# Second output projection of a two-layer decoder trunk: new chunk order, held-back slab sums, and four heads' causal masks moved to another engine

## The chip, the core and the metric

The kernel runs on one core of a Trainium2 chip. The engines of the core work side by side: PE multiplies matrices (its weight loads are listed apart as PEld), DVE is the vector engine, ACT the scalar engine, POOL a third elementwise engine, SP issues most DMAs. Each engine works through its own list of instructions in a fixed order, and an instruction waits until what it reads and overwrites is ready. The metric is the device time of one launch in microseconds (us). A smaller number is better.

## The reference

The model has two layers over 256 tokens of width 2048. The layer that matters here is the second:

```python
sk1, sk2, sv = shared_kv(x, kv_norm, w_kv, k_norm, cos, sin)   # 12 heads, two key maps each, values of 128
u = rms_norm(x, mix_norm[1]) @ w_in[1]
q1, q2 = ...                     # 12 heads of 64: normed, partly rotated
o = differential_attention(q1, q2, sk1, sk2, sv, lam)  # softmax(q1 k1) - lam * softmax(q2 k2), causal, times v
token_out = rms_norm(o, subln_norm[0]) * (1 - lam_init)
mem_out = memory_cross_attention(u[..., 1536:], mem, ...)      # 4 heads of 128, softmax over 256 memory rows
x = x + concatenate([token_out, mem_out]) @ w_out[1]
x = x + squared_relu_mlp(rms_norm(x, ffn_norm[1]), w_ff1[1], w_ff2[1])
```

So the output projection has 16 chunks of 128 input columns: chunks 0 to 11 come from the 12 differential heads, chunks 12 to 15 from the 4 memory heads.

## The kernel before, in words

All weights are float32 and come from HBM once. Every block of weights is split on the core into a rounded high part (ACT, line 157) and the rest (DVE, line 158), and a product is made of three reduced-precision products: high times high and high times low in one matmul of 512 columns (L391), low times high in one of 256 columns (L393). Two rings of six slots (`hi_ring`, `lo_ring`) hold the split blocks. A slot takes four blocks, and it is filled again only after the matmuls of the four blocks before have read it. `Feed` fixes the order of blocks; the split of a later block stands at its place in the fixed lists of ACT and DVE, up to three jobs ahead. Before each feed-forward stage the first slab of the second weight matrix gets sums of two raw tiles (L182 and L183 on DVE); they stand in the list `KOFF` = 2 jobs before the slab.

Work beside the projections is put off by a count of ticks: `at(d, fn)` runs `fn` after `d` ticks, and one tick is four weight blocks. A scheduler then orders each engine's list.

A differential head has four steps. `scores` makes two score tiles (`s1` for the second 128 queries, `s0` for the first), masks, maximum and exponentials. `turn` transposes the weights through bank `t` (`dt`, L1226). `pv` multiplies by the values into bank `o` (`do`, L1232 to L1234) and starts a chain: squares on ACT (L1242), a mean on DVE (L300 `o_v`), two small ACT functions (L359, L360), three small DVE operations ending in `o_y`, and the scaling L1250 on DVE, in two halves. `back` transposes the scaled result (`o_t`, L1255, in two halves) and writes the head's chunk of `cat1`. In the last four heads (8 to 11) `by_pe` is true: the causal mask is added to the scores by PE, as a bf16 matmul with the identity (L1189, L1193), and `pv` first copies the result out of its bank (L1237). The other heads add the mask on DVE (L1202, L1203) and scale straight out of the bank.

A memory head has `scores` (`ms`, L573), a maximum (L575, L576), exponentials on ACT (L579), a reciprocal and a scaling (L584, L586), a turn (`mt`, L592), a copy (L595), `pv` (`mo`, L600) and its chunk of `cat1` in two writes (ACT L601, DVE L602). The score tiles of all heads share two banks; there is one bank `t`, one bank `o`, and there are three banks for the tiles of the projections (tag `mm`).

`out_tiles` makes the 16 output tiles. The first three (called wo0, wo1 and wo2 here) get their chunks in parts while heads are still at work: in the second layer chunks 0 to 7, then 8 to 11, then 12 to 15. Each part runs over the three tiles. A tile's bank is free for the tile three later when `resid_add` (L638, L639) has read it.

Of the kernel before, what the change touches and what calls it, by code (L numbers as in the profile page):

```python
# [19 lines left out]
T = 256  # L20
# [35 lines left out]
class Plan:  # L56
# [7 lines left out]
    def __init__(self):  # L64
        self.entries = []
        self.npos = 0
        self.jobs = []
        self.slabs = []
# [37 lines left out]
class Feed:  # L106


    def __init__(self, nc, wst, wpool, rows, plan, dry):
        self.nc, self.wst, self.wpool, self.rows = nc, wst, wpool, rows  # L110
        self.plan, self.dry = plan, dry
        self.pos = 0
        self.slab_no = 0
        self.lp = self.pp = 0
        self.raw = {}
        self.split = {}
        self.t1 = None
        if not dry:
            self.hi = wpool.tile([P, SLOTS * 512], F32R, name="hi_ring")
            self.lo = wpool.tile([P, SLOTS * 512], F32R, name="lo_ring")  # L120
            self.busy = [False] * SLOTS
            self.at = 0
# [39 lines left out]
    def _prepare(self, p):  # L162
        sub, add = self.nc.vector.tensor_sub, self.nc.vector.tensor_add
        self.load(self.plan.need[p] + 1 + LOADS)
        if p[0] == "N":
            r = ("N", p[1] // 2)
            c = p[1] % 2 * 512
            if not self._split(p, self.raw[r][:, c : c + 512], 1):
                return False
            if c:  # L170
                del self.raw[r]
            return True
        ra, rb = self.raw[("S", p[1], 0)], self.raw.get(("S", p[1], 1))
        t1 = self.t1[1 if p[1] % 32 > 28 else p[1] % 2]

        def both():
            t2 = rb[:, 0:512].unsqueeze(1).to_broadcast([P, 2, 512])
            two = ra.rearrange("p (a c) -> p a c", a=2)
            sub(two, t2, two)

        if p[0] in "KL":
            add(t1, ra[:, 0:512], rb[:, 0:512])  # L182
            sub(rb[:, 0:512], t1, rb[:, 512:1024])  # L183
            if p[0] == "L":
                both()
            return True
        src, n = ((ra, 2), (t1, 1), (rb, 2), (ra, 2))[p[2]]
        if not self._split(p, src, n):
            return False
        if p[2] == 0 and ("K", p[1]) in self.plan.need:  # L190
            both()
        if p[2] == 3:
            del self.raw[("S", p[1], 0)], self.raw[("S", p[1], 1)]
        return True
# [68 lines left out]
def program(ctx, tc, plan, dry, xT, memT, par, lam, cst, wst, yT):  # L263
    nc = tc.nc
    cp = ctx.enter_context(tc.tile_pool(name="cp", bufs=1))
    sp = ctx.enter_context(tc.tile_pool(name="sp", bufs=1))
    wp = ctx.enter_context(tc.tile_pool(name="wp", bufs=1))
    tp = ctx.enter_context(tc.tile_pool(name="tp", bufs=1))
    pp = ctx.enter_context(tc.tile_pool(name="pp", bufs=1, space=PSUM))

    nc.scalar.preload_act_table_set("natural_log_exp_and_others")
    feed = Feed(nc, wst, wp, tp, plan, dry)

    acc = {}

# [20 lines left out]
    def mmt(name):  # L296
        return pp.tile([P, 512], F32, tag="mm", bufs=3, name=name)
# [8 lines left out]
    resid = cp.tile([P, NK, T], F32, name="resid")  # L306
# [70 lines left out]
    def a_part(ps, w, l, n, ks, xs, first=True, last=True, between=None):  # L377


        ks = list(ks)  # L380
        i = 0
        while i < len(ks):
            if between:
                between(i)
            two = []
            for k in ks[i : i + 2 - feed.pos % 2]:
                two.append((i, k % NK, *feed.block((w, l, k, n, 1))))
                feed.used()
                i += 1
            for c, k, hi, lo in two:  # L390
                nc.tensor.matmul(ps, hi, xs[:, k, :], start=first and c == 0, stop=False)  # L391
            for c, k, hi, lo in two:
                nc.tensor.matmul(  # L393
                    ps[:, T : 2 * T], lo, xs[:, k, 0:T], start=False,
                    stop=last and c == len(ks) - 1,
                )
            if feed.pos % 4 == 0:
                tick()
# [53 lines left out]
    def key_rows(ps, cols, d):  # L452

        n = 512 // d
        raw = tp.tile([P, 2, 512], F32, tag="rows", bufs=3, name="krow")
        v = tp.tile([P, 2, n], F32, tag="w16", bufs=6, name="kv")
        for t in range(2):
            nc.scalar.activation(raw[:, t, :], ps[t], AF.Copy, scale=cols[0][:, t : t + 1])
            sq = tp.tile([P, 512], F32, tag="rowsq", bufs=1, name="ksq")
            nc.scalar.activation(sq, raw[:, t, :], AF.Square)  # L460
            nc.vector.tensor_reduce(
                out=v[:, t, :], in_=sq.rearrange("p (h d) -> p h d", d=d), axis=AX.X, op=ALU.add
            )
        v = v.rearrange("p t n -> p (t n)")
        nc.vector.tensor_scalar(out=v, in0=v, scalar1=1.0 / d, scalar2=EPS, op0=ALU.mult, op1=ALU.add)
        y = tp.tile([P, 2 * n], F32, tag="w16", bufs=6, name="ky")
        rsqrt_cols(y, v)
        for t in range(2):
            rows = raw[:, t, :].rearrange("p (h d) -> p h d", d=d)
            yb = y[:, t * n : t * n + n].unsqueeze(2).to_broadcast([P, n, d])  # L470
            nc.vector.tensor_mul(rows, rows, yb)
        return raw
# [163 lines left out]

    def resid_add(ps, n):
        nc.vector.tensor_add(resid[:, n, :], resid[:, n, :], ps[:, 0:T])  # L638
        nc.vector.tensor_add(resid[:, n, :], resid[:, n, :], ps[:, T : 2 * T])  # L639

    def resid_done(n, splits, square=True):
        for dst, g in splits:
            split_gain(dst[:, n, :], resid[:, n, :], gcol(g + n))
        if square:
            add_square("x", resid[:, n, :], n == 0)
# [312 lines left out]
    ps = [mmt("mq0"), pp.tile([P, 512], F32, tag="o", bufs=1, name="mq0")]  # L958
# [14 lines left out]
    for h in range(4):  # L973
        mem_head(
            mq0[:, h, :], y0.rearrange("p (t h) -> p t h", t=2)[:, :, h], mk[:, h, :],
            lambda mb, h=h: mv[:, mb, h * P : h * P + P], ebuf[h % 2], pTb, cat[:, 12 + h, :],
# [51 lines left out]
    def out_tiles(l, cat, lead, ks, fx, between):  # L1028

        first = [mmt("wo") for _ in range(3)]  # L1030
        for i, part in enumerate(lead):
            for n in range(3):
                a_part(first[n], "w_out", l, n, part, cat, first=i == 0, last=False)
        between()
        for n in range(NK):
            if n < 3:
                ps = first[n]
                a_part(ps, "w_out", l, n, ks, cat, first=False)
            else:
                ps = mmt("wo")  # L1040
                a_part(ps, "w_out", l, n, sum(lead, []) + ks, cat)
            resid_add(ps, n)
            resid_done(n, [(fx, G_FFN + 16 * l)])

    group_u(3)
# [50 lines left out]
    def pair_of_banks(c, name):  # L1096
        if c % 2:
            return [pp.tile([P, 512], F32, tag="s", bufs=2, name=name) for _ in range(2)]
        return [mmt(name) for _ in range(2)]
# [3 lines left out]
    for c in range(3):  # L1103
        ps = pair_of_banks(c, "k1")
        b_tile(ps, "w_kv", 0, c, x_kv)
        rows = key_rows(ps, c1, 64)
# [8 lines left out]
    for c in range(3):  # L1115
        ps = pair_of_banks(c + 1, "v1")
# [9 lines left out]
    ps = pair_of_banks(0, "mk1")  # L1126
# [4 lines left out]
    ps = pair_of_banks(1, "mv1")  # L1131
# [7 lines left out]
    def carve(n):  # L1139
        off[0] += n  # L1140
        return att[:, off[0] - n : off[0]]
# [5 lines left out]
    pT1 = carve(512).rearrange("p (a t) -> p a t", a=2)  # L1147

    qb = [[carve(512).rearrange("p (m t) -> p m t", m=2) for _ in range(2)] for _ in range(3)]
    em1 = carve(512).rearrange("p (a t) -> p a t", a=2)  # L1150
# [22 lines left out]
    cat1 = sp.tile([P, NK, 512], F32R, tag="S1", name="cat1")  # L1173
# [90 lines left out]
    for c in range(3):  # L1264
        ps = pair_of_banks(0, "q1")
        b_tile(ps, "w_in_q", 1, c, x_mx)
        rows, v = query_rows(ps, c1, 64)
        rope(rows, qtab)
        y = query_scale(v, c1)
        for i in range(2):  # L1270
            j = 2 * c + i
            q = qb[j % 3]
            at(4 + i, lambda i=i, q=q, rows=rows: turn_queries(rows, 2 * i, q))
            for g in range(2):
                h = 2 * i + g

                diff_head(
                    2 * j + g, q[g], y, *((6 + 4 * h, 8, 4 if c == 0 else 3) if c < 2 else (6 + 2 * h, 6, 3)), c == 2
                )
    for h in range(4):  # L1280
        ps = mmt("mq1")
        c_tile(ps, "w_in", 1, 12 + h, range(NK), x_mx)
        q, y = mem_query(ps[:, 0:T], mqg1, c1)
        mem_head(
            q, y, mk1[:, h, :], lambda mb, h=h: mv1[:, mb, h * P : h * P + P],
            em1, pT1, cat1[:, 12 + h, :], 3,
        )

    fx1 = sp.tile([P, NK, 512], F32R, tag="S0", name="fx1")
    out_tiles(1, cat1, [list(range(8)), list(range(8, 12))], list(range(12, 16)), fx1, flush)  # L1290

    down = ffn(1, fx1, ("S2", "S1"), lambda n: nc.sync.dma_start(yT[:, n, :], resid[:, n, :]))
    down()
# [83 lines left out]
```

## Time and profile before

| | |
|---|---|
| time, median of 3 runs | 2045.21 us (2045.16 to 2045.78) |
| the profiled execution: time | 2044.93 us |
| the profiled execution: span of the profile | 2043.1 us |
| PE busy in the span | 2037.2 us |
| DVE, ACT busy in the span | 1716.2 us, 1349.8 us |

The span runs from the first to the last instruction of the program; 1.83 us of the profiled execution lie outside it. The busy time of PE contains overlaps of neighbouring matmuls and gaps that the modelled ends hide. What a matmul costs is therefore read from start to start: the start of the next minus its own.

### The profile page before, as it was taken

Reading aid. Unit: us, or ns where it says so; the run is one execution under the profiler, and the core shown is the slowest. Engines: PE = TensorE matmul, PEld = TensorE weight load, DVE = VectorE, ACT = ScalarE, POOL = GpSimd, SP = SyncE. Lnnn points to the kernel's source line nnn. Section 1 sums busy time; section 2 is a strip of 40 time slices with the busy share of each in tenths; the row PEclk is TensorE's granted clock in tenths of the full one; section 3 lists DMA queues with packets and bytes.
Section 4 is the critical chain, followed back from the end, with each engine's and each line's share of the span. In section 5 each row is a group of like instructions: output and inputs, shape, how many; then the busy total and the mean of one; then the engine's idle time right before and its main releaser. Section 6 shows DMA issues by size and latency. Waiting matters only on the chain.

```text
span 2043.1 us, 32257 instructions
## 1 busy us (share of the span) xinstructions
PE 2037.2 (100%) x11060; PEld 1755.3 (86%) x11060; DVE 1716.2 (84%) x3215; ACT 1349.8 (66%) x2505; POOL 51.9 (3%) x67
## 2 busy tenths in 40 slices
PE   9999999999999999999999999999999999999999
PEld 8888888888888888888888888888888888888888
DVE  8888889889879978999766687889879978988997
ACT  7765566666666756768665697566657666666764
POOL 0001200000000000000000000310000000000000
PEclk9999999999999999999999999999999999999999
DMA  9556556555555555655565543656555555565564
GB/s 314 178 181 190 188 174 206 197 196 197 186 201 202 189 207 191 207 169 182 194 228 186 170 140 103 196 166 207 196 196 205 186 196 196 186 210 195 196 209 135
DMA packets 110470, 390.75 MB, mean 191 GB/s; under 512 B 12256, under 2 KB 14944, under 8 KB 110304
## 3 DMA queue, kind: packets, MB, share of 16 engines
q1 hardware_dynamic: 110160, 388.59, 57.1%
q8 instruction: 86, 1.41, 0.3%
q14 instruction: 80, 0.66, 0.1%
q10 hardware_dynamic: 144, 0.10, 0.0%
HBM read 386.54 MB, written 2.10 MB: 190 GB/s over the span
## 4 chain that ended last, share of the span: by engine, by line
PE 99%; ACT 1%; DVE 1%; issue 0%
PE x_bank L391 33%; PE x_bank L393 16%; PE wo L391 6%; PE p L746 5%; PE p L747 5%; PE p L748 5%; PE wo L393 3%; PE u L391 2%; PE ff L391 2%; PE u L393 1%; PE k L417 1%; PE k L419 1%; PE v L417 1%; PE k L418 1%; PE v L419 1%; PE v L418 1%
## 5 line engine op out<-in xcount | busy, mean ns | idle before, releaser
L157 ACT CAST hi_ring<-raw 128x512 fp32r<-128x512 f32 x1193 | 736.7, 620 | 529.5 <-PE x_bank L391 308.0
L158 DVE TENSOR_TENSOR lo_ring<-raw,hi_ring 128x512 fp32r<-128x512 f32 x1193 | 817.2, 695 | 206.7 <-ACT hi_ring L157 165.5
L391 PE MATMUL x_bank<-fx,hi_ring 128*128 128x512 f32 x1920 | 602.1, 395 | 0.0
L393 PEld LDWEIGHTS x_bank<-fx,lo_ring 128*128 128x128 f32 x1920 | 361.0, 188 | 83.6
L393 PE MATMUL x_bank<-fx,lo_ring 128*128 128x256 f32 x1920 | 377.4, 278 | 0.0
L391 PEld LDWEIGHTS x_bank<-fx,hi_ring 128*128 128x128 f32 x1920 | 301.4, 189 | 9.3
L391 PE MATMUL x_bank<-z,hi_ring 128*128 128x512 f32 x960 | 301.1, 395 | 0.0
L158 DVE TENSOR_TENSOR lo_ring<-slab,hi_ring 128x1024 fp32r<-128x1024 f32 x188 | 230.1, 1224 | 54.3 <-ACT hi_ring L157 53.6
L157 ACT CAST hi_ring<-slab 128x1024 fp32r<-128x1024 f32 x188 | 196.9, 1047 | 73.1 <-PE x_bank L391 36.2
L393 PEld LDWEIGHTS x_bank<-z,lo_ring 128*128 128x128 f32 x960 | 180.5, 188 | 41.7
L393 PE MATMUL x_bank<-z,lo_ring 128*128 128x256 f32 x960 | 188.8, 278 | 0.0
L391 PE MATMUL wo<-cat,hi_ring 128*128 128x512 f32 x512 | 162.5, 398 | 0.5 <-DVE resid L639 0.5
L391 PEld LDWEIGHTS x_bank<-z,hi_ring 128*128 128x128 f32 x960 | 151.9, 189 | 6.5 <-ACT room L672 0.4
L393 PEld LDWEIGHTS wo<-cat,lo_ring 128*128 128x128 f32 x512 | 95.9, 188 | 21.7
L672 ACT COPY room<-x_bank 128x512 f32<-128x512 f32 x180 | 104.9, 583 | 2.0 <-PE x_bank L393 2.0
L393 PE MATMUL wo<-cat,lo_ring 128*128 128x256 f32 x512 | 101.4, 279 | 0.0
L746 PE MATMUL p<-hi_ring,sit 128*128 128x512 f32 x256 | 100.5, 393 | 0.0
L747 PE MATMUL p<-hi_ring,sit 128*128 128x512 f32 x256 | 100.2, 391 | 0.0
L748 PE MATMUL p<-lo_ring,sit 128*128 128x512 f32 x256 | 99.7, 389 | 0.0
L391 PEld LDWEIGHTS wo<-cat,hi_ring 128*128 128x128 f32 x512 | 79.1, 189 | 2.2 <-PE wo L393 0.9
L717 ACT ACTIVATE room<-room 128x256 f32<-128x256 f32 x128 | 53.2, 416 | 39.1 <-DVE room L300 39.1
L746 PE MATMUL p<-hi_ring,z 128*128 128x512 f32 x192 | 75.2, 392 | 0.0
(313 smaller groups left out, 3102.3 us busy)
## 6 DMA issues: line engine op xcount, KB each, us to landing
raw<-in_w SPq DMA_DIRECT2D x595, 512.0 KB, 4.0
slab<-in_w SPq DMA_DIRECT2D x124, 512.0 KB, 3.3
resid<-in_x SPq DMA_DIRECT2D x8, 256.0 KB, 5.9
room<-in_w SPq DMA_DIRECT2D x4, 512.0 KB, 4.2
memraw<-in_mem SPq DMA_DIRECT2D x4, 512.0 KB, 3.6
out_y<-resid SPq DMA_DIRECT2D x16, 128.0 KB, 1.8
memraw<-in_mem SPq DMA_DIRECT2D x7, 256.0 KB, 6.3
raw<-in_w SPq DMA_DIRECT2D x3, 256.0 KB, 3.5
```

What stands on the lines that cost most here:

```text
L157: self.nc.scalar.copy(hi, src)
L158: self.nc.vector.tensor_sub(lo, src, hi.bitcast(F32))
L391: nc.tensor.matmul(ps, hi, xs[:, k, :], start=first and c == 0, stop=False)
L393: nc.tensor.matmul(ps[:, T : 2 * T], lo, xs[:, k, 0:T], start=False, stop=last and c == len(ks) - 1,)
L417: nc.tensor.matmul(ps[t], xl, hi, start=k == 0, stop=False)
L418: nc.tensor.matmul(ps[t], xh, hi, start=False, stop=False)
L419: nc.tensor.matmul(ps[t], xh, lo, start=False, stop=k == NK - 1)
L672: nc.scalar.copy(x, ps)
L717: at(3, lambda: nc.scalar.activation(stage[i % 8], y[:, 0:T], AF.Square))
L746: nc.tensor.matmul(ps, a[1], hi, start=first, stop=False)
L747: nc.tensor.matmul(ps, a[0], hi, start=False, stop=False)
L748: nc.tensor.matmul(ps, a[0], lo, start=False, stop=last)
```

## The change

Four things are changed.

- The last four heads add their causal mask on DVE like the others (`by_pe` false). The 16 bf16 mask matmuls and the four copies L1237 go; eight mask additions of DVE come.
- The ticks of the last heads and of the memory heads are other: `pv` of heads 8 to 11 comes 7 ticks after their scores (before: 6), the scores of a memory head come after 4 ticks (before: 3) and its `pv` 7 ticks after those (before: 6).
- The chunks of wo0, wo1 and wo2 in the second layer come as 0 to 7, then 12, 8, 9, 13, then 10, 11, 14, then 15.
- The sums L182 and L183 of the first slab of each feed-forward stage are held, by a dependency for the scheduler alone, behind the second addition `resid_add` of the third output tile, in both layers.

```diff
@@ Feed._prepare
         if p[0] in "KL":
-            add(t1, ra[:, 0:512], rb[:, 0:512])
+            one = add(t1, ra[:, 0:512], rb[:, 0:512])
+            if self.gate:
+                self.tc.add_manual_dep(
+                    one.ins, self.gate,
+                    mybir.DependencyInfo(
+                        mybir.DependencyClass.NoSync, mybir.DependencyReason.SCHED_ONLY
+                    ),
+                )
+                self.gate = None
             sub(rb[:, 0:512], t1, rb[:, 512:1024])
@@ resid_add
-        nc.vector.tensor_add(resid[:, n, :], resid[:, n, :], ps[:, T : 2 * T])
+        return nc.vector.tensor_add(resid[:, n, :], resid[:, n, :], ps[:, T : 2 * T])
@@ out_tiles
-            resid_add(ps, n)
+            done = resid_add(ps, n)
+            if n == 2 and not dry:
+                feed.gate = done.ins.name
@@ the differential heads
-                    2 * j + g, q[g], y, *((6 + 4 * h, 8, 4 if c == 0 else 3) if c < 2 else (6 + 2 * h, 6, 3)), c == 2
+                    2 * j + g, q[g], y, *((6 + 4 * h, 8, 4 if c == 0 else 3) if c < 2 else (6 + 2 * h, 7, 3)), False
@@ the memory heads
-            em1, pT1, cat1[:, 12 + h, :], 3,
+            em1, pT1, cat1[:, 12 + h, :], 4, 7,
@@ the second output projection
-    out_tiles(1, cat1, [list(range(8)), list(range(8, 12))], list(range(12, 16)), fx1, flush)
+    out_tiles(1, cat1, [list(range(8)), [12, 8, 9, 13], [10, 11, 14]], [15], fx1, flush)
```

The lists of SP and POOL are the same in both built programs. On PE the lists differ from the scores of head 8 on, up to the end of wo2. In the built programs PE's list stands as follows there, in short (mem is a memory head, "half" is one of the two transposes of a `back`):

```
before                                        after
last query tile of mem 3, in it:              last query tile of mem 3, in it:
  scores 11, pv 8, pv 9, pv 10,                 pv 8, scores 11, back 7
  scores mem 1, pv mem 0, back 7, turn mem 1
scores mem 2                                  wo0: chunks 0 to 3, in it scores mem 1, scores mem 2
wo0: chunks 0 to 7, in it turn 11, pv mem 1   wo0: chunks 4 to 7, in it turn 11
pv 11, in it back 8                           wo1: chunks 0 to 7
wo1: chunks 0 to 7, in it back 9              back 8 (half), pv 9, back 8 (half)
wo0, wo1: chunks 8, 9                         turn mem 1, back 9 (half)
turn mem 2, scores mem 3                      scores mem 3 (half), pv mem 0, back 9 (half), scores mem 3 (half)
wo2: chunks 0 to 7, in it pv mem 2, back 10   wo2: chunks 0 to 7, in it turn mem 2, pv 10, back 10 (half),
back 11                                         pv 11, back 10 (half)
wo0, wo1, wo2: chunks 8 to 15, in it          wo0, wo1, wo2: chunks 12, 8, 9
  turn mem 3, pv mem 3                        back 11 (half), pv mem 1, back 11 (half), turn mem 3 (quarter)
                                              wo0: 13; pv mem 2; wo1: 13; turn mem 3; wo2: 13
                                              wo0, wo1: 10, 11, 14; wo2: 10, 11; pv mem 3; wo2: 14
                                              wo0, wo1, wo2: 15
wo3                                           wo3
```

More of the change, by code (lines that the diff above doesn't have):

```diff
@@ L106, with __init__ @@
 class Feed:
-    def __init__(self, nc, wst, wpool, rows, plan, dry):
-        self.nc, self.wst, self.wpool, self.rows = nc, wst, wpool, rows
+    def __init__(self, tc, wst, wpool, rows, plan, dry):
+        self.tc, self.nc, self.wst, self.wpool, self.rows = tc, tc.nc, wst, wpool, rows
         self.plan, self.dry = plan, dry
@@ L181, in _prepare @@
         if p[0] in "KL":
-            add(t1, ra[:, 0:512], rb[:, 0:512])
+            one = add(t1, ra[:, 0:512], rb[:, 0:512])
[6 more added lines that the diff above has]
+                )
+                self.gate = None
             sub(rb[:, 0:512], t1, rb[:, 512:1024])
@@ L271, in program @@
     nc.scalar.preload_act_table_set("natural_log_exp_and_others")
-    feed = Feed(nc, wst, wp, tp, plan, dry)
+    feed = Feed(tc, wst, wp, tp, plan, dry)
     acc = {}
```

## The prediction

> **What bounds the kernel now.** The page comes first: busy time by engine, and the chain of work that ended last.
>
> ```profile
> PE 2037.2 (100%) x11060; PEld 1755.3 (86%) x11060; DVE 1716.2 (84%) x3215; ACT 1349.8 (66%) x2505; POOL 51.9 (3%) x67
> PE 99%; ACT 1%; DVE 1%; issue 0%
> ```
>
> PE is the end of the chain for 99% of the span, so a change is worth what it takes from PE's work or from PE's waits. Then the windows around the end of the heads, in which PE still shows idle time, and the wait that stands there.
>
> ```profile
> 1260.00:1270.00 10.00, 9.24 (x54) 7.85 (x53) 8.28 (x32) 7.84 (x29) 0.00 (x0) 1.00 0.30 105
> 1280.00:1290.00 10.00, 10.00 (x60) 8.76 (x59) 10.00 (x17) 4.99 (x10) 3.92 (x5) 1.00 0.63 203
> ```
>
> The fields are PE, PEld, DVE and ACT busy, then the granted clock, 1.00. The list of waits has, in this stretch (total us, count, longest):
>
> ```profile
> PE mt L592 <- DVE att L586: 0.8, 1, 0.8
> ```
>
> Busy time hides part of a wait, so the timeline of PE is read from start to start:
>
> ```profile
> 1260.79 0.39 PE L393 MATMUL wo<-cat,lo_ring 128*128 128x256 f32 x2
> 1261.95 0.81 PE L592 MATMUL mt<-const,att 128*128 128x128 f32 x4 [0.76 <-DVE att L586]
> ```
>
> The next matmul starts 1.16 us after the two L393, whose work is 0.23 (by the 0.23 of one of twice the columns, below): a wait of 0.93. That is the largest in this stage. What could be gained here is small, and what can be lost is not bounded by it.
>
> **The masks.** Scores with the mask on DVE and on PE, in PE's timeline:
>
> ```profile
> 1160.47 0.52 PE L1226 MATMUL dt<-const,att 128*128 128x128 f32 x3
> 1160.82 1.03 PE L1197 MATMUL s<-big,att 128*128 128x256 f32 x4
> 1161.69 0.61 PE L1200 MATMUL s<-big,att 128*128 128x128 f32 x4
> 1162.05 0.48 PE L417 MATMUL q<-hi_ring,x_mx 128*128 128x512 f32 x1
> 1162.37 0.40 PE L418 MATMUL q<-hi_ring,x_mx 128*128 128x512 f32 x1
> 1162.60 0.39 PE L419 MATMUL q<-lo_ring,x_mx 128*128 128x512 f32 x1
> ...
> 1219.54 0.60 PE L1188 MATMUL s<-big,att 128*128 128x256 f32 x2
> ...
> 1220.58 0.44 PE L1192 MATMUL s<-big,att 128*128 128x128 f32 x2
> ...
> 1232.34 0.39 PE L1192 MATMUL s<-big,att 128*128 128x128 f32 x2
> ...
> 1232.92 0.37 PE L405 MATMUL mq<-x_mx,hi_ring 128*128 128x256 f32 x1
> ```
>
> Start to start, `s1` takes 0.87 without and 1.04 with the mask matmuls, `s0` 0.36 and 0.58: 0.39 a head, 1.6 us for four heads off PE. The first projection matmul after the float32 ones (1162.05) takes 0.32, the next one 0.23; the built program has five fewer such changes of kind (41 for 46), 0.45 us. PE's work falls by 2.05 us. On DVE eight additions like the next row come, and four copies of the same size go:
>
> ```profile
> 1212.43 0.43 DVE L1202 TENSOR_TENSOR s<-s,const 128x256 f32<-128x256 f32 x1
> ```
>
> That is 1.7 us more of DVE in 60 us. It costs PE nothing where scores of a head have several us of query-tile matmuls behind them, as heads 8 to 10 have; if that cover were gone it would be 0.7 a head, up to 2.8.
>
> **The held sums.**
>
> ```profile
> 1257.39 0.68 DVE L182 TENSOR_TENSOR room<-slab,slab 128x512 f32<-128x512 f32 x1
> 1258.11 0.69 DVE L183 TENSOR_TENSOR slab<-room,slab 128x512 f32<-128x512 f32 x1
> ACT hi_ring L157 <- PE wo L391: 7.4, 11, 1.0
> ```
>
> The two stand ahead of the maximum of memory head 2, whose scaling PE awaits at 1261.95; holding them takes 1.37 us from that chain. They go where DVE is busy throughout (the window 1280 to 1290). But ACT waits there for PE to free ring slots, so splits run about five jobs ahead, some 7 us; 1.37 fits in. I take nought for their new place in both layers; were DVE itself late, up to 1.4 us in each.
>
> **The order.** This is the large term. In the list of the built program some steps now stand shortly behind the step whose result they need. PE cannot pass them. The chain between a `pv` and its `back`, in the lists of ACT and DVE when little else stands there (head 11 before), and where that `back` stood:
>
> ```profile
> 1263.28 0.32 ACT L1242 ACTIVATE o_sq<-osb 128x128 f32<-128x128 f32 x1
> 1265.36 0.48 DVE L1250 TENSOR_SCALAR osb<-osb,o_y 128x128 f32<-128x128 f32 x2
> ```
>
> ```profile
> 1256.36 0.39 PE L1234 MATMUL do<-big,att 128*128 128x128 f32 x2
> 1267.88 0.44 PE L1255 MATMUL o_t<-const,osb 128*128 128x128 f32 x2
> ```
>
> From the squares to the end of the first half of the scaling it is 2.08 + 0.3 = 2.4 us; the transposes came 11.5 us after `pv`, so the chain cost PE nothing.
>
> Two groups of the page, for the splits that stand in these lists:
>
> ```profile
> L157 ACT CAST hi_ring<-raw 128x512 fp32r<-128x512 f32 x1193 | 736.7, 620 | 529.5 <-PE x_bank L391 308.0
> L158 DVE TENSOR_TENSOR lo_ring<-raw,hi_ring 128x512 fp32r<-128x512 f32 x1193 | 817.2, 695 | 206.7 <-ACT hi_ring L157 165.5
> ```
>
> *Head 9 after.* Between `pv` 9 and the first half of `back` 9 stand half of `back` 8 and the turn of memory head 1, five transposes of 0.12 at most (three took 0.35 from 1160.47 on): 0.5 us. ACT has a copy and two small scalings ahead of the squares (about 0.5), and DVE the maximum of memory head 2 ahead of L1250 (0.6, by the row of L575 below less its overlap). 2.4 + 0.5 + 0.6 - 0.5 = 3.0 us of idle PE. Bounds: 1.9 with nothing in between, 3.7 with one more operation of that size ahead. Everything of PE's list waits behind it, wo2 too.
>
> *Head 8.* Its `back` now stands behind wo1's eight chunks, but on DVE its `o_y` stands behind a split whose slot wo1's first four chunks free: 0.62 on ACT, 0.69 on DVE and the scaling make 1.9 to 2.1 us, PE has 1.4 us left of wo1 (four chunks at 0.23 + 0.12). 0.7 us, 0 to 1.5.
>
> *Head 11.* Behind `pv` 11 PE has 3.2 us (a transpose, two chunk products, chunks 12, 8, 9 of three tiles at 0.93 each). On ACT a split, two scalings and the write of head 10 stand ahead of the squares, about 1.6; on DVE a split and small steps delay the mean by 0.55, and the maximum of memory head 3 the scaling by 0.6. 1.6 + 2.4 + 0.55 + 0.6 = 5.15, plus crossings 0.25, less 3.2: 2.2 us, 0 to 2.8. The new chunk order makes this bite: `pv` of memory head 1 needs bank `o` from head 11, and chunk 13 stands ahead of 10 and 11 in each tile, so no other chunk can fill the gap.
>
> *Memory head 3.* Its steps before:
>
> ```profile
> 1268.01 0.68 DVE L575 TENSOR_REDUCE mm_max<-ms 128x2 f32<-128x512 f32 x1
> 1269.46 0.56 ACT L579 ACTIVATE att<-ms,mm_max,mq_y 128x256 f32<-128x256 f32 x1 [0.62 <-DVE mm_max L576]
> 1270.89 0.62 DVE L586 TENSOR_SCALAR att<-att,mm_rec 128x256 f32<-128x256 f32 x2
> 1271.30 0.33 PE L592 MATMUL mt<-const,att 128*128 128x128 f32 x1
> ```
>
> From the exponentials to the turn it is 1.84 us. After the change L576 stands behind head 11's scaling, and PE has only `pv` of memory head 1 (0.7) before the turn's first quarter: 1.2 us. Chunk 13 then waits for its second write, queued behind L586: 0.3. Together 1.5, 0.8 to 2.2. Memory head 2's turn, behind the copy of memory head 1's: 0.3, 0 to 0.6.
>
> *The last chunk, and wo3's bank.* Before:
>
> ```profile
> 1272.96 1.04 PE L600 MATMUL mo<-att,mv 128*128 128x256 f32 x4
> 1274.92 0.50 PE L391 MATMUL wo<-cat,hi_ring 128*128 128x512 f32 x1
> ...
> 1277.29 0.70 PE L391 MATMUL wo<-cat,hi_ring 128*128 128x512 f32 x2 [0.33 <-DVE resid L639]
> ```
>
> Chunk 15 is usable 1.96 us after its `pv` starts. After the change one chunk product lies in between, a few less than before: 0.3 more wait, 0 to 0.7. wo0 then ends two products before wo3: 0.2 more, 0 to 0.4.
>
> **The sum.** 3.0 + 0.7 + 2.2 + 1.5 + 0.3 + 0.3 + 0.2 = 8.2 us of new waits, less 0.93 that goes, less 2.05 of work: +5.2 us. On the profiled execution's 2044.93 (span 2043.1 and 1.83 around it) this is 2050.1; that execution lies 0.28 under the median 2045.21, within the spread of the runs. I forecast 2050.1 us.
>
> The clock is 1.00 in the 1260 to 1270 window, across the 0.93 us wait; the new waits, up to 3.0 us, are longer than any that the trace shows. The Trainium skill, "TensorE: Matmul & The Clock Gate", section "HAM oscillation — how this bites in real kernels", lets the clock fall to half once PE idles over about 3.4 us. By it the sum stays as it is, with a wait just under that mark; an estimate from that page for one that passes it is 3.4 us at half speed, 1.7 us more.
>
> **Rivals.** *ACT and DVE are ahead of my count.* The chains behind heads 9 and 11 take their lower ends (1.9 and 0), head 8 none, memory head 3 0.8, the rest 0.3 in all: 3.0 of new waits less 2.98, no change, 2045 us; halfway to the forecast 2047.5. For it: I add queue delays that partly overlap, and DVE is busy 8.28 of 10 us in that window, not all. Against: the lists are fixed, and head 9's minimum alone is 1.9. Chance 0.35 for +0.5 to +4.1.
>
> *Not slower.* PE's work falls by 2.05 and the 0.93 wait goes, with every new chain covered by PE work: 2044.93 - 2.98, or 2042 us. The place is `back` 9; it decides if that chain takes under 0.5 us where the trace's quick case is 2.4. Chance 0.08, a fifth of it for more than 4.1 us.
>
> *The clock falls after a long wait.* If waits of 3 us lower the granted clock for some us, the matmuls behind them cost twice 0.23: per 3 us at half speed 1.5 us, with two such waits 3 us, 2053 us. For it: the waits are three times the longest seen here. Against: no window here is under 1.00. Chance 0.05. It follows the rule of the page named above.
>
> That the change does not do what it says is excluded by the built program: no mask matmul is left.
>
> **Numbers.** 0.2% is 4.09 us, about what a measurement of this kernel can tell from no change. Forecast case (+4.1 to +7.5) 0.52, clock 0.05, smaller waits 0.35, not slower 0.08. Slower by over 0.2%: 0.52 + 0.05 = 0.57. Within 0.2%: 0.35 + 0.06 = 0.41. Faster: 0.02. All lower ends give about 2044.7, all upper ends (3.7, 1.5, 2.8, 2.2, 0.6, 0.7, 0.4: 11.9 less 2.98) 2053.8; ends that all fall together are rare, so the range is 2043.8 to 2052.8, with a tenth or less on either side. For slower alone it is 2049.3 to 2052.8.
>
> **What would show it.** After the change, L1189, L1193 and L1237 are gone; PE's waits between 1235 and 1285 us name L1255 on DVE's L1250 twice, some 2.5 and 2 us, and L592 on L586, 1 us; the first wo3 matmul starts 5 us later than 1277.29; windows from 1300 on are as full as before, and the clock is 1.00. Wrong would be a wait of `back` 9 under 1 us, a clock below 1.00, or PE waits after 1290, which would say that the held sums or DVE are late.

## The result, and the profile after

The changed kernel takes 2051.08 us (median of 8 runs, 2049.78 to 2053.43), the kernel before 2045.65 us beside it (8 runs, 2045.16 to 2046.0). The ratio is 1.0027, with a 95% interval of 1.0018 to 1.0036: 5.4 us slower. The forecast was 2050.1 us, slower, within 2043.8 to 2052.8. The profiled execution of the changed kernel took 2051.26 us, with a span of 2049.5. Line numbers are now 10 to 12 higher: the scaling is L1262, `back` L1267, the turn of a memory head L602, its `pv` L610, the squares L1254.

From the page of the changed kernel, the engines and the chain that ended last:

```profile
PE 2038.5 (99%) x11044; PEld 1754.3 (86%) x11044; DVE 1717.2 (84%) x3219; ACT 1349.5 (66%) x2505; POOL 52.4 (3%) x67
PE 98%; ACT 1%; DVE 0%; DMA 0%; issue 0%; SPq 0%
```

PE has 16 instructions fewer and is still the chain, so the loss is idle PE or slower PE. The list of PE's waits in the changed kernel from 1200 to 1310 us (total us, count, longest):

```profile
PE o_t L1267 <- DVE osb L1262: 3.5, 3, 2.2
...
PE wo L401 <- DVE resid L649: 0.6, 1, 0.6
PE wo L401 <- DVE cat L612: 0.6, 1, 0.6
```

The transposes of `back` wait three times for the scaling; the two 0.6 are the last chunk and wo3's bank. In PE's timeline, with the idle time and its releaser in brackets:

```profile
1254.57 0.30 PE L1267 MATMUL o_t<-const,osb 128*128 128x128 f32 x1 [0.37 <-DVE osb L1262]
1254.74 0.49 PE L1244 MATMUL do<-big,att 128*128 128x128 f32 x2
...
1255.51 0.27 PE L1267 MATMUL o_t<-const,osb 128*128 128x128 f32 x1
1256.24 0.66 PE L602 MATMUL mt<-const,att 128*128 128x128 f32 x4 [0.46 <-ACT att L1239]
1259.09 0.31 PE L1267 MATMUL o_t<-const,osb 128*128 128x128 f32 x1 [2.19 <-DVE osb L1262]
1259.23 1.03 PE L583 MATMUL ms<-att,mq 128*128 128x256 f32 x2
1260.05 1.91 PE L610 MATMUL mo<-att,mv 128*128 128x256 f32 x4
...
1271.84 0.30 PE L1267 MATMUL o_t<-const,osb 128*128 128x128 f32 x1 [0.95 <-DVE osb L1262]
1272.00 1.13 PE L610 MATMUL mo<-att,mv 128*128 128x256 f32 x4
...
1283.58 0.70 PE L401 MATMUL wo<-cat,hi_ring 128*128 128x512 f32 x2 [0.59 <-DVE resid L649]
```

Two things stand here. First, `pv` 9 (L1244, 1254.74) comes only after the scaling of head 8, and `back` 9 (1259.09) only after that of head 9: a chain from head to head. Second, four matmuls of the kind L610 take 1.91 us at 1260.05 and 1.13 at 1272.00. The windows show why (us, busy time of PE, PEld, DVE, ACT and POOL, then the granted clock, DMA share and GB/s):

```profile
1250.00:1256.00 6.00, 5.42 (x34) 4.46 (x32) 5.25 (x20) 4.52 (x16) 0.00 (x0) 1.00 0.40 133
1256.00:1259.00 3.00, 0.66 (x4) 0.42 (x4) 2.08 (x9) 2.10 (x10) 0.00 (x0) 1.00 0.23 89
1259.00:1260.00 1.00, 0.91 (x3) 0.81 (x4) 0.27 (x2) 0.64 (x3) 0.00 (x0) 0.62 0.00 0
1260.00:1261.00 1.00, 1.00 (x4) 0.77 (x3) 0.30 (x2) 0.56 (x3) 0.00 (x0) 0.50 0.00 0
1261.00:1262.00 1.00, 1.00 (x5) 0.71 (x4) 0.22 (x1) 0.00 (x0) 0.00 (x0) 0.50 0.00 0
1262.00:1263.00 1.00, 1.00 (x5) 0.84 (x5) 0.60 (x2) 1.00 (x3) 0.00 (x0) 0.67 0.00 0
...
1290.00:1300.00 10.00, 10.00 (x59) 8.71 (x59) 9.19 (x16) 5.16 (x9) 3.41 (x4) 1.00 0.58 195
```

Behind 3 us with 0.66 of PE work the granted clock is 0.50 for 3.4 us; the four windows lose 0.38 + 0.50 + 0.50 + 0.33 = 1.7 us. It does not happen in every run: three of the eight have a mean granted clock of 1.000 and take 2049.78 to 2050.03, four have 0.999 (2050.90 to 2051.86), one has 0.998 (2053.43). The changed kernel's spread of 3.6 us, against 0.8 before, is this.

From 1290 us on PE is full, as before.

### The profile page after: what moved, and what is told of

It is laid out like the page before. It is cut to its first block, busy times and chain, and to the rows that moved or that the text cites. A ratio compares the mean times of both kernels' runs of the same rounds, so it can differ in the third digit from the quotient of the medians.

```text
span 2049.5 us, 32234 instructions
## 1 busy us (share of the span) xinstructions
PE 2038.5 (99%) x11044; PEld 1754.3 (86%) x11044; DVE 1717.2 (84%) x3219; ACT 1349.5 (66%) x2505; POOL 52.4 (3%) x67
## 4 chain that ended last, share of the span: by engine, by line
PE 98%; ACT 1%; DVE 0%; DMA 0%; issue 0%; SPq 0%
PE x_bank L401 33%; PE x_bank L403 16%; PE wo L401 6%; PE p L756 5%; PE p L757 5%; PE p L758 5%; PE wo L403 3%; PE u L401 2%; PE ff L401 2%; PE u L403 1%; PE k L427 1%; PE v L429 1%; PE k L429 1%; PE k L428 1%; PE v L427 1%; PE v L428 1%
```

## Why the steps close up: the bank

PE's timeline of the changed kernel shows `pv` 8, ACT's and DVE's show the squares and the scaling that read its bank:

```profile
1239.63 0.42 PE L1244 MATMUL do<-big,att 128*128 128x128 f32 x2
1239.89 0.39 PE L1245 MATMUL do<-big,att 128*128 128x128 f32 x2
1240.11 0.39 PE L1246 MATMUL do<-big,att 128*128 128x128 f32 x2
```

```profile
1250.94 0.27 ACT L1254 ACTIVATE o_sq<-do 128x128 f32<-128x128 f32 x1
```

```profile
1254.07 0.61 DVE L1262 TENSOR_SCALAR osb<-do,o_y 128x128 f32<-128x128 f32 x2
...
1258.60 0.60 DVE L1262 TENSOR_SCALAR osb<-do,o_y 128x128 f32<-128x128 f32 x2
```

The only bank `o` is held from 1239.6 to 1254.7, some 15 us, because ACT comes to the squares late in its list and the scaling now reads the bank (`osb<-do`). The kernel before copies it out first; the view of the tile `do` from 1240 to 1262 us has it:

```profile
L1237 DVE COPY osb<-do x3: 414/418/425, 1242.6 to 1252.2; 128x256 f32<-128x256 f32 x3
```

With that copy `pv` 9, 10 and 11 need not wait for any scaling: `pv` 11 stands at 1256 us before, at 1267 after. No wait of the changed kernel's PE names the bank itself; what the hold costs there is, by this reading, the place that the later steps got in the list, each behind the scaling of the head before. The prediction listed these four copies as DVE time that is saved; that they free the bank it did not price. This became the theory that the runs below had to decide, against: late ticks alone, the chunk order, the held sums, or DVE made late by the masks.

## The experiments

Each is compared with the kernel before on the same chip (medians 2045.88, 2045.75 and 2045.67 in the three groups; 2045.65 beside the changed kernel). The clock named is each run's mean granted clock.

### One part undone at a time

**u_ticks**, the ticks of before:

```diff
-                    2 * j + g, q[g], y, *((...) if c < 2 else (6 + 2 * h, 7, 3)), False
+                    2 * j + g, q[g], y, *((...) if c < 2 else (6 + 2 * h, 6, 3)), False
...
-            em1, pT1, cat1[:, 12 + h, :], 4, 7,
+            em1, pT1, cat1[:, 12 + h, :], 3,
```

> The changed kernel with the ticks of before (pv of the last heads after 6 ticks, memory heads 3 and 6); masks on DVE, new chunk order and held sums stay. Before is at 2045.65 us, the changed kernel at 2051.08. Theory (late ticks put the steps shortly behind the chains they need): in the list pv 9 now stands 30 PE instructions ahead of back 9 and pv 11 some 27 ahead of back 11, so the waits of 2.35 and 1.11 us go; the mask work of 2 us is still saved: 2043 to 2045. Rival A (the chunk order costs): 2049 to 2051. Rival B (the held sums make DVE late): 2050 to 2051.

Measured: 2055.62 us, ratio 1.0046 (1.0033 to 1.0058), 4.5 us slower than the changed kernel. All three expectations missed. PE's timeline of this kernel:

```profile
1252.23 1.13 PE L610 MATMUL mo<-att,mv 128*128 128x256 f32 x4 [1.72 <-DVE osb L1262]
```

`back` no longer waits, but `pv` of the first memory head waits 1.72 us for head 8's scaling, which it can only need for the bank. The long distance between `pv` 9 and `back` 9 in the list helps nothing, since `pv` 9 itself is late. Waits of this kind come to 1.9 us in this kernel; 4.8 us are other waits, 1.7 of them for the scalings of memory heads. So the late ticks are not the cause; with the copy gone they help.

**u_order**, the chunk order of before:

```diff
-    out_tiles(1, cat1, [list(range(8)), [12, 8, 9, 13], [10, 11, 14]], [15], fx1, flush)
+    out_tiles(1, cat1, [list(range(8)), list(range(8, 12))], list(range(12, 16)), fx1, flush)
```

> The changed kernel with the chunk order of before (0 to 7, 8 to 11, 12 to 15). Theory (ticks): back 9 still stands shortly behind pv 9 (two chunk products more in between, 0.35 us), pv 11 still 14 products ahead of back 11: waits of about 2.0 and 1.1 us stay, 2049 to 2051. Rival A (the chunk order costs, since chunk 13 stands ahead of 10 and 11): both waits shrink and the time is 2043 to 2046.

Measured: 2048.67 us, ratio 1.0015 (1.0007 to 1.0024); nine of eleven runs at clock 1.000. Between the two ranges, nearer to the first. The largest of its PE's waits from 1235 to 1290 us:

```profile
PE o_t L1267 <- DVE osb L1262: 2.3, 3, 1.2
```

The same chains are there, `back` 11's longer than with the new order (1.2 for 0.95). `back` 9 runs at 1259.21 in this profile, 1259.09 in the other: two chunk products merely fill 0.46 us of its wait. That is enough to keep the clock up in most runs, and the two waits before wo3 (0.6 each) are gone. These three make about the 2.4 us by which this kernel is faster than the changed one. So without the copy the new order costs; it is not what closes the list.

**u_masks**, the masks on PE, and the copy with them:

```diff
-                    2 * j + g, q[g], y, *((...) if c < 2 else (6 + 2 * h, 7, 3)), False
+                    2 * j + g, q[g], y, *((...) if c < 2 else (6 + 2 * h, 7, 3)), c == 2
```

> The changed kernel with the masks of the last four heads on PE again, and with them the copy of the result out of its bank behind pv; late ticks, new chunk order and held sums stay. Theory as predicted (late ticks alone put back behind pv): the waits of back 9 and back 11 stay, plus 2 us of mask work: 2050 to 2053. Refined theory (it takes late ticks and the missing copy together: without the copy the next pv needs the bank that the scaling still reads, and the list closes up): in this list back 9 stands 19 PE instructions behind pv 9 and back 11 over 30 behind pv 11, no long wait is left, the last chunk costs 0.5 us more and the 0.93 us wait is gone: 2045 to 2046.

Measured: 2045.65 us, ratio 1.0000 (0.9991 to 1.0008), clock 1.000 in all eleven runs. As the refined theory had it for this run; its other half, that the late ticks are needed for the loss, is refuted by u_ticks. All that PE waits for from 1235 to 1290 us:

```profile
PE wo L401 <- DVE resid L649: 0.6, 1, 0.6
PE wo L401 <- DVE cat L612: 0.6, 1, 0.6
```

**u_held**, without the hold on the slab sums:

```diff
             if n == 2 and not dry:
-                feed.gate = done.ins.name
+                pass
```

> The changed kernel without the hold on the slab sums: PE's list is the same as in the changed kernel, the two sums go back into DVE's list ahead of the last maximum. Theory: the sums then stand in a chain that PE awaits, up to 1.4 us more: 2051 to 2053. Rival B (the held sums make DVE late in the feed-forward): 2048 to 2050, with the PE waits after 1280 us smaller.

Measured: 2053.79 us, ratio 1.0037 (1.0025 to 1.0049): 2.7 us more than with the hold, above the 1.4 us expected at most for the sums. PE's timeline:

```profile
1272.90 0.30 PE L1267 MATMUL o_t<-const,osb 128*128 128x128 f32 x1 [1.83 <-DVE osb L1262]
```

`back` 11 waits 0.9 us longer, since the sums stand ahead of its scaling. The rest is the clock: in this profile it is 0.50 a second time, behind this wait, for 6.8 us, and the run times go with it: one at 1.000 took 2050.66 us, two at 0.999 took 2052.48 and 2052.78, three at 0.997 over 2054.8. (The intervals of the two ratios overlap; the 0.9 us are read from the profiles.)

### The copy, and one part alone

**masks_alone**, the kernel before with the masks on DVE:

```diff
-                    2 * j + g, q[g], y, *((...) if c < 2 else (6 + 2 * h, 6, 3)), c == 2
+                    2 * j + g, q[g], y, *((...) if c < 2 else (6 + 2 * h, 6, 3)), False
```

> The kernel before, with the masks of the last four heads on DVE and nothing else changed (so the copy of the result out of its bank goes too). By the prediction's sum (the ticks and the order cost, the mask move saves 2.05 us): 2043.5 to 2044. By the theory that the missing copy costs (the bank of pv is now held until the scaling has read it, some 3 us, and the next pv waits for that on PE): PE waits of 1 to 2 us name L1262's line (the scaling) at pv of a memory head, as with the ticks undone, the clock falls in most runs: 2052 to 2056.

Measured: 2051.85 us, ratio 1.0029 (1.0017 to 1.0040), clock 0.999 in four of six runs. Hardly below the theory's range, and 8 us off the other. PE's waits from 1235 to 1290 us:

```profile
PE wo L401 <- DVE cat L310: 2.2, 2, 1.4
PE mo L610 <- DVE osb L1262: 1.9, 2, 1.7
```

The second line is the bank; the first is heads' chunks of `cat1` that come too late for wo0 to wo2. That these are late for the bank alone is not shown: with the copy (masks_copy, below) 1.6 us of such a wait remain.

**copy_away_alone**, the kernel before without the copy, masks still on PE:

```diff
-            if by_pe:
-                nc.vector.tensor_copy(osb, o)
-                o = osb
```

> The kernel before with one thing changed: the last four heads do not copy the result of pv out of its bank, so squares and scaling read the bank itself. Masks on PE, ticks, chunk order and slab sums as before. Theory (the held bank is the cause): pv of the first memory head, pv 9, pv 10 and the next memory heads' pv each wait for the scaling of the step before; about the loss of masks_alone (6.1 us) plus the 2 us that the masks there save: 2051 to 2055. Rival (taking masks to DVE costs, by DVE's eight additions): a DVE copy less, 2044.5 to 2046.

Measured: 2049.77 us, ratio 1.0022 (1.0013 to 1.0031), clock 1.000 in eight of eleven runs. 4.1 us slower by taking work away: the rival is out, and the size is 1.2 us short of the theory's range. Only 0.2 us of wait names the bank here:

```profile
PE wo L391 <- DVE cat L300: 1.4, 2, 0.8
...
PE mo L600 <- DVE osb L1247: 0.2, 1, 0.2
```

The rest is late chunks. Every later `pv` has moved: `pv` 9 stands at 1254.3 us (1245.7 before), `pv` 11 at 1268.2 (1255.7), and the delay comes out at the end of the chain. That the scheduler moved them because it knows that the bank is held is argued; the copy is the only thing that differs.

**copy_kept**, the changed kernel in full, with the copy (masks on DVE):

```diff
-            if by_pe:
+            if by_pe or by_copy:
                 nc.vector.tensor_copy(osb, o)
...
-                    2 * j + g, q[g], y, *((...) if c < 2 else (6 + 2 * h, 7, 3)), False
+                    2 * j + g, q[g], y, *((...) if c < 2 else (6 + 2 * h, 7, 3)), False, c == 2
```

> The changed kernel in full (late ticks, chunk order, held sums, masks on DVE), but the last four heads copy the result of pv out of its bank on DVE again before the chain, as the kernel before does. Theory (missing copy): the list opens up again (back 9 stands 25 PE instructions behind pv 9, back 11 some 60 behind pv 11), the waits of 0.5, 0.6, 2.35 and 1.1 us go, the 2 us of mask work stay saved, the last chunk's 0.8 us stay: 2043.5 to 2045, clock 1.000 in all runs. Rival (late ticks by themselves, or DVE late): the long waits stay at back 9 and back 11, 2049 to 2052.

Measured: 2045.70 us, ratio 0.9999 (0.9991 to 1.0008), clock 1.000 in all eleven runs. The copy alone takes the whole 5.4 us back, as the theory had it; but the time is 0.7 us over its range, so the 2 us of mask work do not show. PE's waits from 1235 to 1285 us:

```profile
PE mt L602 <- DVE att L596: 0.8, 1, 0.8
PE wo L401 <- DVE resid L649: 0.6, 1, 0.6
PE wo L401 <- DVE cat L612: 0.6, 1, 0.6
PE o_t L1267 <- DVE osb L1262: 0.2, 1, 0.2
```

Against u_masks, which differs only in who adds the masks, there are two more waits on DVE's results, 0.92 and 0.32 us from start to start. These take back 1.24 us of the saving. `pv` 11 stands at 1257.5 us again.

**copy_kept_old_order**, copy_kept with the edit of u_order:

> As the one before (copy kept, masks on DVE, late ticks, held sums), with the chunk order of before. Theory: PE has eight products more between the last pv and the last chunk's first use, so the waits of 0.74 and 0.75 us there shrink to about 0.2 in all: 1 us under the one before, 2042.5 to 2044. Rival (the new chunk order helps): 2044 to 2046.

Measured: 2046.98 us, ratio 1.0006 (0.9997 to 1.0016). The theory's gain did not come; the rival was nearer. With the copy in place the new order is worth about 1.3 us (the slowest of copy_kept's eleven runs took 2046.75, the quickest of these 2046.4), and with it the clock was 1.000 in every run, here in two of eleven: `back` 11 and the turn of memory head 3 now wait one behind the other.

**order_alone**, the kernel before with the edit of u_order turned round:

> The kernel before with the new chunk order alone (0 to 7, then 12, 8, 9, 13, then 10, 11, 14, then 15). By the prediction's terms (0.3 us at the last chunk, 0.2 at wo3, and the 0.93 us wait of memory head 2's turn covered by more chunk products ahead of it): 2045 to 2046.3. By what the changed kernel shows (0.74 and 0.75 us at these two places, where before had 0.29 and 0.49): 2045.5 to 2046.5. Rival (the order is the large term, +4 us and more): over 2049.

Measured: 2047.89 us, ratio 1.0011 (1.0002 to 1.0020), above the first two ranges and below the rival's. PE's waits from 1235 to 1285 us:

```profile
PE wo L401 <- DVE cat L310: 1.2, 1, 1.2
PE wo L401 <- DVE cat L612: 0.9, 1, 0.9
```

The first line is a head's chunk of `cat1` that its new place in the order asks for before its second write is done. So the new order is a gain of 1.3 us with the copy, the late ticks and the held sums together, and a loss of 2.2 us on the kernel before and of 2.4 without the copy (u_order).

**masks_copy** and **masks_copy_held**: the kernel before with the masks on DVE and the copy kept (the edit of masks_alone and that of copy_kept), without and with the held sums of the change.

> The kernel before with the masks of the last four heads on DVE, and the copy out of the bank kept; ticks, order and slab sums as before. Theory (masks save 2.05 us of PE, the copy keeps the bank short): 2043.3 to 2045, clock 1.000. Rival (DVE gets late by eight additions): the wait of memory head 2's turn grows past 1.5 us, 2045 to 2047.

> As masks_copy, with the slab sums held back. Theory: the two sums (1.4 us) leave the chain ahead of the last memory heads' maximum, so 0.5 to 0.9 us less than masks_copy: 2042.5 to 2044.3. Rival (their new place costs as much): within 0.2 us of masks_copy, or above.

Measured: 2048.53 us, ratio 1.0015 (1.0006 to 1.0024), and 2046.22 us, ratio 1.0003 (0.9994 to 1.0011). Both above their ranges; for the first the rival (DVE late) is right in kind, by another wait, which the second more than halves. So at the old ticks the move of the masks costs 2.9 us by itself, and 6.1 when the copy goes too (masks_alone): there the copy accounts for 3.2 us, about half. PE's waits on a head's chunk, first without and then with the hold:

```profile
PE wo L401 <- DVE cat L310: 1.6, 1, 1.6
```

```profile
PE wo L401 <- DVE cat L310: 0.6, 1, 0.6
```

The hold is worth 0.9 us of wait here too (1.56 and 0.63 before rounding), and 2.3 us of time: without it the clock is below 1.000 in eight of eleven runs, with it in none.

### The clock

**clock_fill**, the changed kernel with useless work in its longest wait:

```diff
-            for mb in range(2):
+            for mb in [0, 1] * (1 + again):    # again = 3 for memory head 1
```

> The changed kernel with the four transposes of memory head 1's turn done four times over: 12 useless matmuls, 1.3 us of PE work, in the place where PE waits 2.35 us for back 9. Theory (a long idle stretch makes the granted clock fall for 3 us): the idle stretch is cut to about 1 us, the clock stays 1.000 in all runs, and the time is that of the changed kernel's undisturbed runs, 2049.5 to 2050.2, with a spread under 1 us in place of 3.6. Rival (the half speed has nothing to do with the idle time): the clock is 0.999 or 0.998 in most runs and the median stays at 2051 or rises to 2052.4 by the added work.

Measured: 2049.93 us, ratio 1.0023 (1.0013 to 1.0032), 2049.24 to 2051.88. Twelve more transposes, 1.3 us of PE work, and no time lost: the median is 1.1 us under the changed kernel's (the intervals overlap). Seven of ten runs are at clock 1.000 (three of eight without the filling), but not all as expected. Its windows, from a run at 0.999:

```profile
1259.00:1260.00 1.00, 1.00 (x7) 0.87 (x6) 0.00 (x0) 1.00 (x4) 0.00 (x0) 1.00 0.00 0
...
1273.00:1274.00 1.00, 1.00 (x5) 0.91 (x4) 0.21 (x2) 0.62 (x1) 0.00 (x0) 0.50 0.00 0
```

Behind the filled place the clock is 1.00; it falls at the next pair of waits, `back` 11 and memory head 3, which was not filled. One profile does not show how often it falls at which place; the shift in the counts is small, and with these windows it speaks for idle PE as what lowers the clock.

The traces' own record of the granted clock shows more. In every trace of this case the clock changes only at whole multiples of 3.413 us after its first rise, and each fall, but for one in the last microseconds of a program, lasts one such step or two: in the changed kernel one, from 1259.25 to 1262.66 us, in u_held one and then two. The step ahead of the fall, 1255.84 to 1259.25 us, has 0.82 us of PE work. The same waits can lie within one step or be split between two, as the steps happen to start, which would explain why only some runs of a program have a fall. No threshold comes out of these traces: a step with 1.69 us of PE work has no fall behind it in masks_alone, one with 2.11 us has.

No version measured is shown to beat the kernel before; copy_kept, u_masks, masks_copy_held and copy_kept_old_order cannot be told from it by their intervals.

## Why the prediction was right, and where not

**Time and direction** hold, but in part by two errors that cancel, which is luck. From the same matmul of the query tiles (at 1216.71 us before, at 1217.37 after) to the first one of wo3 (1277.29, 1283.58) the stage is 5.6 us longer: 60.6 us, then 66.2. The forecast was 5.2 of waits less work, at a clock of 1.00. The runs at clock 1.000 lie 4.2 us above before, so waits less work were over-counted by about 1 us; the clock that fell in five of eight runs puts the median 1.3 us higher.

**The terms**, from start to start in the profile after:

| term | predicted us | measured us |
|---|---|---|
| head 9, `pv` to `back` | 3.0 | 2.35 |
| turn of memory head 1 behind `pv` 9 | none | 0.62 |
| head 8 `back` | 0.7 | 0.53 |
| head 11 `pv` to `back` | 2.2 | 1.11 |
| memory head 3's turn and chunk 13 | 1.5 | 1.0 |
| memory head 2's turn | 0.3 | 0 |
| last chunk | 0.3 | 0.7 |
| wo3's bank | 0.2 | 0.26 |
| sum of new waits | 8.2 | 6.6 |

With the 0.93 us wait gone (it is), 2.05 us of PE work less and 1.7 us of half clock, 6.6 gives 5.3 of the 5.6; 0.3 stays unassigned, or the work fell by 1.7 only. The reading from PE's list, ACT's and DVE's queues and the chain of 2.4 us gave waits in the right places, those of `back` named by the right pair (L1262 ahead of L1267). For memory head 3 the pair was another: PE's turn was released by ACT's copy L605 of memory head 2's turn, which stands behind the exponentials and ends at 1274.03, and the scaling that the prediction named was done 0.2 us before. The size that failed is head 11's, half its price: the first rival said that queue delays on ACT and DVE were added up though they overlap, and its lower end of 0 for this chain was too low as well. The 0.25 us for crossings in head 11's term comes from no row; in the trace after, `back` 11 starts 0.15 us behind the end of its scaling. Head 9's 3.0 came in two pieces: 0.62 at the turn of memory head 1, which waits for the copy L1239 behind `pv` 9, and 2.35 at `back` 9.

**The cause that was missing.** The prediction put the closing up to the list's order and said that the new chunk order makes head 11 bite. u_order shows the same waits without that order, u_ticks and masks_alone show more loss without the late ticks, and copy_kept shows none with the copy. What failed is the step on the masks, which set the four copies off against four of DVE's eight additions and did not see in them the release of the only bank; the built list was read rightly, without asking what had closed it up. With the copy gone, the late ticks (4.5 us, u_ticks) and the held sums (2.7, u_held) repair a part and the new order adds 2.4 (u_order): masks_alone is 6.1 us slower than before, the full change 5.4. These amounts are each measured in the changed kernel and do not simply add up. That the copy acts through the bank rests on the waits that name it (u_ticks, masks_alone) and on the places of `pv`; no run gave `o` a second bank, which would show it by itself.

**The held sums** were right: 1.37 us off a chain that PE awaits was the estimate; 0.9 us at `back` 11 (u_held) and 0.9 at a head's chunk (masks_copy_held) were measured, and from 1290 us on nothing shows that their new place costs.

**The masks' cover.** 2.05 us of PE work were taken as saved. In copy_kept they do not arrive: from the same `back` (1204.99 us in u_masks, 1204.31 here) to wo3 (1278.88, 1277.99) it takes 73.9 us with the masks on PE and 73.7 with them on DVE. 1.24 us return as waits on DVE, where the prediction had said that eight additions cost PE nothing, and some 0.6 of the 2.05 is not seen. The waits stand at 1269 to 1271 us, long after the additions have run; that these delay the chain up to there is argued and not shown. At the old ticks the cover is worse: masks_copy is 2.9 us slower than before, and 1.5 in its runs at clock 1.000.

**The clock rival** had a chance of 0.05 and 1.5 us for each fall; the size is right (1.7), the chance was far too low. The condition was put to a single wait of 3 us. In the trace the longest wait is 2.19 us, with 0.46 and 0.37 shortly ahead of it and 0.66 us of transposes in between. The Trainium skill, "TensorE: Matmul & The Clock Gate", section "HAM oscillation — how this bites in real kernels", says no idle gaps above some 3.4 us; the trace disagrees for a single gap, since the clock fell where the longest was 2.19 us. The Trainium skill, same page, section "Part 1: The HAM clock gate (the "warmup" mystery)", says that the activity window is free-running and the outcome varies from run to run: the runs agree (three of eight without a fall), and the half-speed stretch of 3.41 us is the 3.4 that it gives for the window.

## What to carry to other kernels

A copy that looks like overhead may be what frees a buffer: when an edit removes one, find what holds the buffer next, until when, and who writes it next; here the bank was held for 2.4 us, until the copy had run, and for some 15 us without it. A list that a scheduler has made says where steps stand, not why; if the built list closes up, ask which buffer closed it before blaming the order. Count idle PE over stretches of some 3.4 us, not wait by wait, because several short waits together can cost 1.7 us more through the clock.

## What was not expected of the hardware

A stretch of 3.41 us in which PE has 0.82 us of work was followed by a granted clock of 0.50 for 3.41 us, though no single wait exceeds 2.2 us; this happens in some runs of the same program and not in others (times of 2049.8, 2051 and 2053.4 us for none, one and, by the mean clock, two such steps). In every trace here the clock changes only at whole multiples of 3.413 us after its first rise. With twelve useless transposes in the stretch the clock behind it was 1.00 in the profile, and the kernel no slower.
